# Decay rows of a bidirectional SSD encoder: stored by unit, both directions side by side, and fetched in 4 KB runs

## The chip, the cores and the metric

The kernel runs on one core of a Trainium2 chip. A core has a matrix engine (PE in the profile, with PEld for its weight loads), a vector engine (DVE), a scalar engine (ACT), GpSimd (POOL) and a queue engine (SP) that issues nearly all transfers between device memory and on-chip memory; 16 DMA engines carry them. Each engine works through its own list of instructions in order and waits on semaphores for the others. The metric is device microseconds (us) of one execution, lower is better. Before the change three runs gave 3012.8, 3020.76 and 3021.59 us; the median is 3020.76 us.

## What is computed

One encoder layer is applied to two sequences, 1024 and 2048 tokens, 1024 wide, all in float32. The input is normed and multiplied by a large matrix `w_in`. One part of the product goes through a Fourier mixing branch, another through a state-space branch that runs over the tokens in both directions; the two are gated, joined, projected and added to the input. The change concerns the state-space branch, computed in chunks of 128 tokens:

```
a = (dt * A)                                  # per token and head, one set for each direction
a_cs = cumsum(a, axis=chunk)
seg = a_cs[:, :, :, None] - a_cs[:, :, None, :]
decay = exp(where(lower triangle, seg, -inf))
cb = einsum('bclgn,bcsgn->bclsg', Cc, Bc)
y_diag = einsum('bclsg,bclsgr,bcsgrp->bclgrp', cb, decay, X)
...                                           # states of the chunks, carried from chunk to chunk
y_off = einsum('bclgn,bcgrpn,bclgr->bclgrp', Cc, prev, exp(a_cs))
y = y_fwd + flip(y_bwd) + D * xs              # 24 heads of 64 channels, in 4 groups
```

For each head, direction and chunk the kernel needs two rows of 128 numbers: `a_cs` along the chunk, laid over all 128 partitions (for `decay`), and `exp(a_cs)`, laid over the head's 64 partitions (for `y_off`). These are the decay rows.

## The kernel before, in words

The tokens are worked on in three blocks of 1024 (P for the first sequence, S1 and S2 for the second). In each block the projection is done in columns of 128 channels: a Job loads a 512 KB slice of `w_in` (`weights_in`, L182, one buffer `wr`), ACT rounds it into a high part `wh` (L189), POOL forms the rest `wl` (L190), and PE multiplies in three pieces of 342 tokens, 24 matmuls a piece (L361). One piece is a step. Everything else is hung on numbered steps, `pre` ahead of the step's matmuls or `post` behind them, and each engine gets its instructions in that order. So the order of the work on every engine, the SP queue included, is written out by these step numbers; no engine can take a later thing first.

The 24 heads are handled two at a time as 12 units, of 128 channels each. Ahead of the units, `dt_rows` turns the sums of a block into `rows` and `erow`, which hold one head and direction per partition (forward heads on partitions 0 to 23, backward on 32 to 55), and `dt_out` (L499, L500) writes both to device memory, as `ROWd` and `EXPd` in the order chunk, head, token. From there they are read back with each row repeated over many partitions, which is what `bcast_rows` does. `Unit.plan` places the work of a unit:

- four times (p = 0 to 3, two chunks each): `rows_in` asks for the rows of both directions (L540, tiles `R0` and `R1`, one request each), two steps later `rows_cut` masks them on POOL (L548), one step after that `rows_exp` takes eight exponentials on ACT (L558), then `rows_joined` adds the directions and multiplies by `cb` on DVE (L563, L564), and `diag` uses the result on PE (L575)
- `weighted` on POOL (L587, tile `xw`) and `states` on PE (L607, tile `pst`) and DVE (L614, L618): the states of the chunks
- twice (chunks 0 to 3 and 4 to 7): `decays` asks for the exponentiated rows (L635, tiles `er0` and `er1`, two requests for each direction), `across` uses them on DVE (L652), `gated` finishes on POOL (L658; in S1 also L662 and L663), `out` stores (L667, L669)

While block P or S1 is running, the input of the next one is brought in: `load_x` (L122, tile `xt`) for the sums of squares on ACT (L719), and again at the end of the block for the norm on DVE (L250) and the turn on PE (L264).

After the three blocks come the Fourier stage and two stages with the remaining products (from L839 on), which the change doesn't touch.

Of the kernel before, what the change touches and what calls it, by code (L numbers as in the profile page):

```python
# [9 lines left out]
F32 = mybir.dt.float32  # L10
# [8 lines left out]
P = 128  # L19
# [37 lines left out]
def tile_hybrid_encoder(ctx: ExitStack, tc: tile.TileContext, a):  # L57
# [37 lines left out]
    def bcast_rows(src, n):  # L95
        return src.partition_broadcast(n)
# [5 lines left out]
    with ExitStack() as ph:  # L102
# [61 lines left out]
        wdt = cp.tile([P, KT, 2, 64], F32R, name="wdt")  # L164

        def dt_weights_in():
            wdr = sp.tile([P, KT, 64], F32, tag="R1", bufs=3, name="wdr")
# [70 lines left out]
        def x_normed(b, i, xn):  # L238

            xt, n = xn  # L240
            if b["n"] == "P":
                junk = sp.tile([P, DM], BF16, tag="R0", bufs=3, name="junk")
# [7 lines left out]
            V.scalar_tensor_tensor(xt[:n, :], xt[:n, :], rs, nwb[:n, :], op0=ALU.mult, op1=ALU.mult)  # L250
# [175 lines left out]
        def dt_turned(B):  # L426
            B.pv = sp.tile([P, NCH, 64], F32, tag="xw", name="pv")
            for c4 in range(0, NCH, 4):
# [3 lines left out]
                S.copy(B.pv[:, c4:c4 + 4, :], pt[:, :, 0:64])  # L432
                V.tensor_tensor(B.pv[:, c4:c4 + 4, :], pt[:, :, 64:128], B.pv[:, c4:c4 + 4, :], op=ALU.add)

        def dt_softplus(B, part):

            pv = B.pv
            if part:
                dtm, dmx, de, dz = B.sp
                for m in (9, 7, 5, 3):  # L440
                    V.scalar_tensor_tensor(dtm, dtm, 1.0 / m, dz, op0=ALU.add, op1=ALU.mult)
                V.scalar_tensor_tensor(dtm, dtm, 1.0, de, op0=ALU.add, op1=ALU.mult)
                V.scalar_tensor_tensor(dtm, dtm, 2.0, dmx, op0=ALU.mult, op1=ALU.add)
# [4 lines left out]
            dtm = sp.tile([P, NCH, 64], F32, tag="R1", bufs=3, name="dtm")  # L448
            dmx = sp.tile([P, NCH, 64], F32, tag="R0", bufs=3, name="dmx")
            de = sp.tile([P, NCH, 64], F32, tag="R0", bufs=3, name="de")  # L450
            dz = sp.tile([P, NCH, 64], F32, tag="R1", bufs=3, name="dz")
# [44 lines left out]
            B.rows, B.erow = rows, erow  # L496

        def dt_out(B):
            nc.sync.dma_start(ROWd[B.bi].rearrange("c h l -> h c l"), B.rows)  # L499
# [25 lines left out]
        class Unit:  # L525
# [6 lines left out]


            def rows_in(self, p):
                B, u, cc = self.B, self.u, 2 * p
                self.R[p] = []
                for d in range(2):
                    hc = 32 * d + 2 * u
                    R = sp.tile([P, 2, 2, P], F32, tag=f"R{d}", bufs=3, name=f"R{d}")
                    nc.sync.dma_start(  # L540
                        R.rearrange("p c h l -> p c (h l)"),
                        bcast_rows(ROWd[B.bi][cc:cc + 2, hc:hc + 2, :].rearrange("c h l -> c (h l)"), P))
                    self.R[p].append(R)

            def rows_cut(self, p):
                for d, R in enumerate(self.R[p]):
                    sgn = 1 if d == 0 else -1
                    G.affine_select(  # L548
                        out=R.rearrange("p c h l -> p (c h) l"), in_=R.rearrange("p c h l -> p (c h) l"),
                        pattern=[[0, 4], [sgn, P]], compare_op=ALU.is_ge, fill=NEG, base=0,  # L550
                        channel_multiplier=-sgn)

            def rows_exp(self, p):
                for d, R in enumerate(self.R[p]):
                    hc = 32 * d + 2 * self.u
                    for c in range(2):
                        for h in range(2):
                            S.activation(R[:, c, h, :], R[:, c, h, :], AF.Exp,  # L558
                                         bias=self.B.lb[:, 2 * p + c, hc + h:hc + h + 1])

            def rows_joined(self, p):
                E = self.R[p]
                V.tensor_tensor(E[0], E[0], E[1], op=ALU.add)  # L563
                V.tensor_tensor(E[0], E[0],  # L564
                                self.B.cb[self.g][:, 2 * p:2 * p + 2, :].unsqueeze(2).broadcast_to([P, 2, 2, P]),
                                op=ALU.mult)

            def diag(self, p):

# [3 lines left out]
                for c in range(2):  # L573
                    for h in range(2):
                        T.matmul(pd[h * 64:h * 64 + 64, c2 + c, :],  # L575
                                 lhsT=self.xm[c4][:, c2 + c, h * 64:h * 64 + 64],
                                 rhs=self.R[p][0][:, c, h, :], start=True, stop=True)
                if p % 2:
                    self.y[c4] = y = sp.tile([P, 4, P], F32, tag="y0", name="y")
                    V.scalar_tensor_tensor(y.rearrange("p c l -> p (c l)"), self.xT[:, c4 * P:(c4 + 4) * P],  # L580
# [58 lines left out]
            def across(self, c4):  # L639

# [3 lines left out]
                for d in (1, 0):  # L644
                    cs = [c for c in range(4) if B.entered(d, c4 + c)]
                    cr = slice(cs[0], cs[-1] + 1)
                    po = bank([P, 4, P], f"po{d}")
                    for c in cs:
                        T.matmul(po[:, c, :], lhsT=self.H[d][:, c4 + c, :],
                                 rhs=B.CT[self.g][:, (c4 + c) * P:(c4 + c + 1) * P], start=True, stop=True)  # L650
                    t = sp.tile([P, 4, P], F32, tag="y1", bufs=1, name="yt")
                    V.tensor_tensor(t[:, cr], po[:, cr], self.er[d, c4][:, cr], op=ALU.mult)  # L652
                    V.tensor_tensor(y[:, cr], y[:, cr], t[:, cr], op=ALU.add)  # L653

            def gated(self, c4):
# [2 lines left out]
                G.tensor_tensor(yf, yf, zT[:, tk], op=ALU.mult)  # L658
                if self.B.b["n"] == "S1":

                    er_b = self.er[1, c4]
# [9 lines left out]
            def plan(self, s0):  # L671
# [714 lines left out]
```

## Time and profile before

| What | Value |
|---|---|
| median of three runs | 3020.76 us |
| the profiled execution, by its own time | 3021.5 us |
| its span from first to last instruction | 3019.7 us |
| PE, PEld, DVE, ACT, POOL busy | 94%, 85%, 73%, 46%, 49% of the span |
| mean granted clock of PE | 0.974 |
| DMA packets, bytes | 454578, 440.54 MB |
| three blocks with the units | about 130 to 1950 us |
| Fourier stage and remaining products | about 1950 us to the end |

A share of busy time is a mean over the whole span. PE is the engine nearest to full; where it is idle, the views of waits and the timeline name what ended each wait. The row of windows gives, for a stretch of time, the busy time of each engine, the clock granted to PE (1.00 is full), the busy share of the 16 DMA engines and the bytes that they moved. The rows themselves stand in the prediction.

### The profile page before, as it was taken

The page shows a single profiled execution, that of the slowest core. Times are in us where ns is not written, and L with a number is a line of the kernel's source. Part 1 is how long each engine was busy: PE and PEld are TensorE (multiplying, and loading weights), DVE is VectorE, ACT ScalarE, POOL GpSimd, SP SyncE. Part 2 cuts the span into 40 slices and gives each one's busy share as a digit, 9 for nine tenths or more (in the row PEclk, how much of TensorE's full clock was granted, in tenths as well). Part 3 has the DMA queues.
Part 4 walks back from the last instruction along what each step waited for, and adds up shares of the span by engine and source line. Part 5 has one row for each costly group of instructions (what it writes and reads, how often), then busy time and mean ns, then how long its engine had stood idle before and what let it go on. Part 6 is the DMA issues. An engine that isn't in the chain of part 4 may idle for free. (4 is left out here: it accounts for less than half of the span.)

```text
span 3019.7 us, 47067 instructions
## 1 busy us (share of the span) xinstructions
PE 2831.3 (94%) x17252; PEld 2570.1 (85%) x17252; DVE 2217.9 (73%) x3412; ACT 1389.5 (46%) x2980; POOL 1488.2 (49%) x1114
## 2 busy tenths in 40 slices
PE   6999999989999989989999999978899899989998
PEld 6899999989999889989999999867677677768887
DVE  3687777666778667666868777687989888866665
ACT  4544545434545454434544444334433533355554
POOL 1255646432567566542556564455787688610000
PEclk9999999999999999999999999979999999999999
DMA  3388877872789779853677687666553654352221
GB/s 97 77 130 160 167 156 170 139 142 78 143 163 171 164 188 155 160 153 74 122 164 144 154 160 137 127 217 235 168 181 130 231 166 147 126 199 91 94 85 69
DMA packets 454578, 440.54 MB, mean 146 GB/s; under 512 B 24384, under 2 KB 405444, under 8 KB 450508
## 3 DMA queue, kind: packets, MB, share of 16 engines
q1 hardware_dynamic: 454060, 436.50, 61.5%
q8 instruction: 136, 2.23, 0.3%
q14 instruction: 94, 0.77, 0.1%
q10 hardware_dynamic: 288, 1.05, 0.1%
HBM read 328.41 MB, written 110.10 MB: 145 GB/s over the span
## 5 line engine op out<-in xcount | busy, mean ns | idle before, releaser
L361 PE MATMUL ps<-uh,wh 128*128 128x342 f32 (+1 forms) x2880 | 962.3, 334 | 11.7 <-ACT uh L267 8.5
L361 PE MATMUL ps<-ul,wh 128*128 128x342 f32 (+1 forms) x2880 | 926.1, 322 | 2.5 <-DVE ul L268 2.5
L361 PE MATMUL ps<-uh,wl 128*128 128x342 f32 (+1 forms) x2880 | 927.2, 322 | 0.9 <-POOL wl L190 0.9
L190 POOL TENSOR_TENSOR wl<-wr,wh 128x1024 fp32r<-128x1024 f32 x120 | 298.9, 2491 | 712.2 <-ACT wh L189 698.6
L361 PEld LDWEIGHTS ps<-uh,wh 128*128 128x128 f32 x2880 | 551.2, 191 | 35.3 <-issue 16.0
L361 PEld LDWEIGHTS ps<-ul,wh 128*128 128x128 f32 x2880 | 553.6, 192 | 4.2 <-DVE ul L268 3.5
L361 PEld LDWEIGHTS ps<-uh,wl 128*128 128x128 f32 x2880 | 549.8, 191 | 1.7 <-POOL wl L190 1.6
L558 ACT ACTIVATE R<-R,lb 128x128 f32<-128x128 f32 x1152 | 356.1, 391 | 89.5 <-POOL R L548 88.0
L548 POOL TENSOR_SCALAR_AFFINE_SELECT R<-R 128x512 f32<-128x512 f32 x288 | 270.4, 954 | 117.0 <-DMA R<-ROWd 113.0
L618 DVE SCALAR_TENSOR_TENSOR H<-H,cd,pst 128x64 f32<-128x64 f32 x888 | 182.7, 275 | 92.6 <-PE pst L607 90.4
L587 POOL TENSOR_TENSOR xw<-xm,wd 128x512 f32<-128x512 f32 x144 | 188.6, 1319 | 74.1 <-ACT xm L423 62.5
L1102 PE MATMUL X<-whP,ah 128*128 128x512 f32 x480 | 195.2, 407 | 7.8 <-ACT pu L1111 5.4
L402 DVE SCALAR_TENSOR_TENSOR xT<-raw,cvt,xT 128x1024 f32<-128x1024 f32 x144 | 197.3, 1370 | 2.6
L367 ACT COPY raw<-ps 128x342 f32<-128x342 f32 x180 | 78.3, 438 | 252.9 <-PE ps L361 247.9
L1102 PE MATMUL X<-whP,al 128*128 128x512 f32 x480 | 192.1, 400 | 2.1 <-DVE al L1073 2.1
L1102 PE MATMUL X<-wlP,ah 128*128 128x512 f32 x480 | 193.1, 402 | 0.5 <-DVE wlP L861 0.5
L1214 POOL TENSOR_TENSOR ht<-ht,pu 128x512 f32<-128x512 f32 x96 | 155.4, 1627 | 62.9 <-ACT pu L1111 39.9
L607 PE MATMUL pst<-xw,Bm 128*128 128x128 f32 x1056 | 146.4, 281 | 28.6 <-POOL xw L587 28.6
L607 PEld LDWEIGHTS pst<-xw,Bm 128*128 128x128 f32 x1056 | 137.5, 195 | 33.8 <-POOL xw L587 33.6
L563 DVE TENSOR_TENSOR R<-R,R 128x512 f32<-128x512 f32 x144 | 141.3, 981 | 31.4 <-ACT R L558 28.8
L1073 DVE TENSOR_TENSOR al<-s,ah 128x512 fp32r<-128x512 f32 x144 | 143.6, 1019 | 20.2 <-ACT ah L1072 20.0
L653 DVE TENSOR_TENSOR y<-y,yt 128x512 f32<-128x512 f32 (+1 forms) x144 | 154.6, 1073 | 4.9
(264 smaller groups left out, 5665.4 us busy)
## 6 DMA issues: line engine op xcount, KB each, us to landing
R<-ROWd SPq DMA_DIRECT2D x288, 256.0 KB
wr<-in_w_in SPq DMA_DIRECT2D x120, 512.0 KB
er<-EXPd SPq DMA_DIRECT2D x288, 128.0 KB
Hd<-ht SPq DMA_DIRECT2D x48, 512.0 KB
ht<-Hd SPq DMA_DIRECT2D x48, 512.0 KB
y<-Yd SPq DMA_DIRECT2D x46, 512.0 KB
wlP<-WSd SPq DMA_DIRECT2D x21, 1024.0 KB
Yd<-y SPq DMA_DIRECT2D x72, 256.0 KB
```

The source lines that it names most:

```text
L190: G.tensor_tensor(wl, raw, wh.bitcast(F32), op=ALU.subtract)
L361: T.matmul(ps[:, :n], lhsT=wt[:, kt, :], rhs=ut[:, kt, :n], start=(i == 0), stop=(i == 3 * KT - 1))
L402: V.scalar_tensor_tensor(dst, raw[:, k:k + TB], cvt[:, 20 * k + ct:20 * k + ct + 1], dst, op0=ALU.mult, op1=ALU.add)
L548: G.affine_select(out=R.rearrange("p c h l -> p (c h) l"), in_=R.rearrange("p c h l -> p (c h) l"), pattern=[[0, 4], [sgn, P]], compare_op ...
L558: S.activation(R[:, c, h, :], R[:, c, h, :], AF.Exp, bias=self.B.lb[:, 2 * p + c, hc + h:hc + h + 1])
L587: G.tensor_tensor(xw, self.xm[c4].rearrange("p c (h e) -> p c h e", h=2), col(self.B.wd[:, c4:c4 + 4, hc:hc + 2]).broadcast_to([P, 4, 2, 6 ...
L607: T.matmul(pst[:, c, :], lhsT=B.Bm[self.g][:, c4 + c, :], rhs=xw[:, c, :, :].rearrange("p h e -> p (h e)"), start=True, stop=True)
L618: V.scalar_tensor_tensor(dst[:, e], H[d][:, cc, e], B.cd[:, cc, hc + h:hc + h + 1], pst[:, c, e], op0=ALU.mult, op1=ALU.add)
L653: V.tensor_tensor(y[:, cr], y[:, cr], t[:, cr], op=ALU.add)
L1073: V.tensor_tensor(al, src, ah.bitcast(F32), op=ALU.subtract)
L1102: T.matmul(ps, lhsT=at[:, k, :], rhs=wt[:, k, :], start=(first and i == 0), stop=(i == 11), skip_group_check=not first)
L1214: return lambda t: G.tensor_tensor(h, h, t, op=ALU.add)
```

## The change

`ROWd` and `EXPd` change their order in device memory. `ROWd` becomes [pair of chunks, head, direction, 256 numbers] and `EXPd` [half of the chunks, head, direction, 512 numbers], so that what one step of a unit reads (two heads, both directions, two chunks; or one head, both directions, four chunks) is one run of 4 KB. `rows_in` then makes one request of 512 KB into one tile `R` in place of two of 256 KB; `decays` makes two requests of 256 KB for a half of the chunks, into one tile `er`, in place of four of 128 KB. `dt_out` needs four requests in place of two. Inside `R` the order of a partition's numbers is head, direction, chunk, token, where it was chunk, head, token in a tile for each direction. The masks, the sum and the product take one direction of `R`, two runs of 256 numbers. The pools hold three `R` of 4 KB for three each of `R0` and `R1` of 2 KB; some small tiles that shared those buffers (`junk`, `wdr`, and the four tiles of `dt_softplus`, now two pairs) move with them.

```diff
-    ROWd = [dram.tile([NCH, 64, P], F32, name=f"ROWd{i}") for i in range(3)]
-    EXPd = [dram.tile([NCH, 64, P], F32, name=f"EXPd{i}") for i in range(3)]
+    ROWd = [dram.tile([4, 24, 2, 2 * P], F32, name=f"ROWd{i}") for i in range(3)]
+    EXPd = [dram.tile([2, 24, 2, 4 * P], F32, name=f"EXPd{i}") for i in range(3)]
...
+        def pair_of(name):
+            t = sp.tile([P, 2, NCH, 64], F32, tag="R", bufs=3, name=name)
+            return t[:, 0], t[:, 1]
...
         def dt_out(B):
-            nc.sync.dma_start(ROWd[B.bi].rearrange("c h l -> h c l"), B.rows)
-            nc.sync.dma_start(EXPd[B.bi].rearrange("c h l -> h c l"), B.erow)
+            for d in range(2):
+                for kept, src, n in ((ROWd, B.rows, 2), (EXPd, B.erow, 4)):
+                    nc.sync.dma_start(kept[B.bi][:, :, d, :].rearrange("p h x -> h p x"),
+                                      src[32 * d:32 * d + 24].rearrange("h (p c) l -> h p (c l)", c=n))
...
             def rows_in(self, p):
-                B, u, cc = self.B, self.u, 2 * p
-                self.R[p] = []
+                R = sp.tile([P, 2, 2, 2, P], F32, tag="R", bufs=3, name="R")
+                nc.sync.dma_start(
+                    R.rearrange("p h d c l -> p (h d c l)"),
+                    bcast_rows(ROWd[self.B.bi][p, 2 * self.u:2 * self.u + 2].rearrange("h d x -> (h d x)"), P))
+                self.R[p] = R
+
+            def rows_cut(self, p):
                 for d in range(2):
-                    hc = 32 * d + 2 * u
-                    R = sp.tile([P, 2, 2, P], F32, tag=f"R{d}", bufs=3, name=f"R{d}")
-                    nc.sync.dma_start(
-                        R.rearrange("p c h l -> p c (h l)"),
-                        bcast_rows(ROWd[B.bi][cc:cc + 2, hc:hc + 2, :].rearrange("c h l -> c (h l)"), P))
-                    self.R[p].append(R)
...
             def rows_joined(self, p):
-                E = self.R[p]
+                E = [self.R[p][:, :, d].rearrange("p h c l -> p h (c l)") for d in range(2)]
                 V.tensor_tensor(E[0], E[0], E[1], op=ALU.add)
...
-            def decays(self, d, c4):
-
-                hc = 32 * d + 2 * self.u
-                er = sp.tile([P, 4, P], F32, tag=f"er{d}", bufs=2, name=f"er{d}")
+            def decays(self, c4):
+
+                er = sp.tile([P, 2, 4, P], F32, tag="er", bufs=2, name="er")
                 for h in range(2):
-                    nc.sync.dma_start(er[h * 64:h * 64 + 64],
-                                      bcast_rows(EXPd[self.B.bi][c4:c4 + 4, hc + h, :], 64))
-                self.er[d, c4] = er
+                    nc.sync.dma_start(
+                        er[h * 64:h * 64 + 64].rearrange("p d c l -> p (d c l)"),
+                        bcast_rows(EXPd[self.B.bi][c4 // 4, 2 * self.u + h].rearrange("d x -> (d x)"), 64))
+                self.er[c4] = er
...
-                for d in (1, 0):
-                    pre(s0 + 11, self.decays, d, 0)
-                    pre(s0 + 13, self.decays, d, 4)
+                pre(s0 + 11, self.decays, 0)
+                pre(s0 + 13, self.decays, 4)
```

Each engine's list can be read from the two programs. First the SP queue in block P, from the last step of unit 0 to the first steps of unit 1, before the change (`R` are the rows for the masks, `er` the exponentiated rows, `wr` a slice of `w_in`; behind the arrow stands the source, then the shape; x2 means twice in a row):

```order
L540 DMA R_1225<-ROWd_67 128x2x256
L540 DMA R_1227<-ROWd_67 128x2x256
L635 DMA er_1272<-EXPd_70 64x4x128 x2
L635 DMA er_1275<-EXPd_70 64x4x128 x2
L182 DMA wr<-in_w_in 128x8x128
L635 DMA er_1386<-EXPd_70 64x4x128 x2
L635 DMA er_1389<-EXPd_70 64x4x128 x2
L540 DMA R_1400<-ROWd_67 128x2x256
L540 DMA R_1402<-ROWd_67 128x2x256
L540 DMA R_1494<-ROWd_67 128x2x256
L540 DMA R_1496<-ROWd_67 128x2x256
L182 DMA wr<-in_w_in 128x8x128
```

The same place of the SP queue after the change:

```order
L540 DMA R<-ROWd_67 128x1024
L633 DMA er<-EXPd_70 64x1024 x2
L182 DMA wr<-in_w_in 128x8x128
L633 DMA er<-EXPd_70 64x1024 x2
L540 DMA R<-ROWd_67 128x1024 x2
L182 DMA wr<-in_w_in 128x8x128
```

The places of `wr` among them are the same; between two of them stand half as many requests, each with twice the bytes. Second, POOL in the same block, around two masks (`wl` is the low part of the weights, `xw` the weighted inputs of the states, `ws` a part of later weights). Before:

```order
L190 TENSOR_TENSOR wl<-wr,wh 128x1024
L548 AFFINE_SELECT R_2227<-R_2227 128x512
L548 AFFINE_SELECT R_2229<-R_2229 128x512
L217 TENSOR_TENSOR ws<-wb 128x256
L218 TENSOR_TENSOR ws<-wb,ws 128x256
L190 TENSOR_TENSOR wl<-wr,wh 128x1024
```

After:

```order
L190 TENSOR_TENSOR wl<-wr,wh 128x1024
L549 AFFINE_SELECT R<-R 128x2x256 x2
L217 TENSOR_TENSOR ws<-wb 128x256
L218 TENSOR_TENSOR ws<-wb,ws 128x256
L190 TENSOR_TENSOR wl<-wr,wh 128x1024
```

Nothing moved; the two masks now work on one tile, in two runs of 256. On PE, ACT and DVE the lists have the same operations in the same places as well.

More of the change, by code (lines that the diff above doesn't have):

```diff
@@ L166, in dt_weights_in @@
         def dt_weights_in():
-            wdr = sp.tile([P, KT, 64], F32, tag="R1", bufs=3, name="wdr")
+            wdr = sp.tile([P, KT, 64], F32, tag="R", bufs=3, name="wdr")
             V.memset(wdr, 0.0)
@@ L241, in x_normed @@
             if b["n"] == "P":
-                junk = sp.tile([P, DM], BF16, tag="R0", bufs=3, name="junk")
+                junk = sp.tile([P, DM], BF16, tag="R", bufs=3, name="junk")
                 ss = sp.tile([P, 1], F32, tag="ss", name="ss")
@@ L447, in dt_softplus @@
                 return
[L448 to L451, printed above, removed]
+            dtm, dmx = pair_of("dtm")
+            de, dz = pair_of("de")
             V.tensor_scalar(dmx, pv, 0.0, None, op0=ALU.max)
@@ L534, in rows_in @@
             def rows_in(self, p):
-                B, u, cc = self.B, self.u, 2 * p
-                self.R[p] = []
-                for d in range(2):
-                    hc = 32 * d + 2 * u
-                    R = sp.tile([P, 2, 2, P], F32, tag=f"R{d}", bufs=3, name=f"R{d}")
-                    nc.sync.dma_start(
-                        R.rearrange("p c h l -> p c (h l)"),
-                        bcast_rows(ROWd[B.bi][cc:cc + 2, hc:hc + 2, :].rearrange("c h l -> c (h l)"), P))
-                    self.R[p].append(R)
-            def rows_cut(self, p):
-                for d, R in enumerate(self.R[p]):
+                R = sp.tile([P, 2, 2, 2, P], F32, tag="R", bufs=3, name="R")
[4 more added lines that the diff above has]
+            def rows_cut(self, p):
+                for d in range(2):
+                    R = self.R[p][:, :, d]
                     sgn = 1 if d == 0 else -1
[L548 to L551, printed above, removed]
+                    G.affine_select(out=R, in_=R, pattern=[[0, 2], [0, 2], [sgn, P]], compare_op=ALU.is_ge, fill=NEG,
+                                    base=0, channel_multiplier=-sgn)
             def rows_exp(self, p):
-                for d, R in enumerate(self.R[p]):
+                R = self.R[p]
+                for d in range(2):
                     hc = 32 * d + 2 * self.u
@@ L557, in rows_exp @@
                         for h in range(2):
-                            S.activation(R[:, c, h, :], R[:, c, h, :], AF.Exp,
+                            S.activation(R[:, h, d, c, :], R[:, h, d, c, :], AF.Exp,
                                          bias=self.B.lb[:, 2 * p + c, hc + h:hc + h + 1])
             def rows_joined(self, p):
-                E = self.R[p]
+                E = [self.R[p][:, :, d].rearrange("p h c l -> p h (c l)") for d in range(2)]
                 V.tensor_tensor(E[0], E[0], E[1], op=ALU.add)
-                V.tensor_tensor(E[0], E[0],
-                                self.B.cb[self.g][:, 2 * p:2 * p + 2, :].unsqueeze(2).broadcast_to([P, 2, 2, P]),
-                                op=ALU.mult)
+                cb = self.B.cb[self.g][:, 2 * p:2 * p + 2, :].rearrange("p c l -> p (c l)")
+                V.tensor_tensor(E[0], E[0], cb.unsqueeze(1).broadcast_to([P, 2, 2 * P]), op=ALU.mult)
             def diag(self, p):
@@ L576, in diag @@
                                  lhsT=self.xm[c4][:, c2 + c, h * 64:h * 64 + 64],
-                                 rhs=self.R[p][0][:, c, h, :], start=True, stop=True)
+                                 rhs=self.R[p][:, h, 0, c, :], start=True, stop=True)
                 if p % 2:
@@ L651, in across @@
                     t = sp.tile([P, 4, P], F32, tag="y1", bufs=1, name="yt")
-                    V.tensor_tensor(t[:, cr], po[:, cr], self.er[d, c4][:, cr], op=ALU.mult)
+                    V.tensor_tensor(t[:, cr], po[:, cr], self.er[c4][:, d, cr], op=ALU.mult)
                     V.tensor_tensor(y[:, cr], y[:, cr], t[:, cr], op=ALU.add)
@@ L659, in gated @@
                 if self.B.b["n"] == "S1":
-                    er_b = self.er[1, c4]
+                    er_b = self.er[c4][:, 1]
                     G.tensor_tensor(er_b, er_b, col(elt[:, c4:c4 + 4, self.u]).broadcast_to([P, 4, P]), op=ALU.mult)
```

## The prediction, made before the changed kernel ran

> **What bounds the kernel now.** I read the page first.
>
> ```profile
> PE 2831.3 (94%) x17252; PEld 2570.1 (85%) x17252; DVE 2217.9 (73%) x3412; ACT 1389.5 (46%) x2980; POOL 1488.2 (49%) x1114
> ...
> R<-ROWd SPq DMA_DIRECT2D x288, 256.0 KB
> ...
> er<-EXPd SPq DMA_DIRECT2D x288, 128.0 KB
> ```
>
> PE is busy 94% of the span, so a faster transfer pays only where PE stands still or runs slowly. Next comes the split of the span into windows: start and end, length, busy time of PE, PEld, DVE, ACT and POOL, granted clock, DMA share, GB/s. The middle row is the stage that the change touches.
>
> ```profile
> 0.00:130.00 130.00, 100.35 (x599) 95.47 (x600) 66.83 (x96) 58.82 (x105) 18.82 (x15) 0.95 0.31 82
> 130.00:1950.00 1820.00, 1755.49 (x12235) 1695.42 (x12234) 1317.48 (x2246) 862.16 (x1968) 979.09 (x757) 0.98 0.74 146
> 1950.00:3019.70 1069.70, 975.46 (x4422) 779.17 (x4421) 833.58 (x1071) 468.48 (x909) 490.30 (x343) 0.96 0.45 153
> ```
>
> In this stage PE is idle for 1820 - 1755.49 = 64.5 us, and its clock is not always full. That is all there is to win. What ended the idle time is in the view of PE's waits for the same window (total, times, longest):
>
> ```profile
> PE pst L607 <- POOL xw L587: 28.6, 18, 6.9
> PE pt L264 <- DVE H L618: 13.6, 4, 5.6
> PE pt L264 <- DVE xt L250: 6.3, 2, 5.7
> PE ptt L421 <- DVE y L580: 4.6, 2, 3.3
> PE pd L575 <- issue: 3.3, 1, 3.3
> ```
>
> No transfer is named, so each has to be followed back. The longest `pst` wait, from the timelines of ACT, POOL and PE (start, length; in brackets the idle time and what ended it):
>
> ```profile
> 1117.11 1.05 ACT L189 CAST wh<-wr 128x1024 fp32r<-128x1024 f32 x1 [6.22 <-DMA wr<-in_w_in]
> ...
> 1118.24 2.35 POOL L190 TENSOR_TENSOR wl<-wr,wh 128x1024 fp32r<-128x1024 f32 x1 [4.47 <-ACT wh L189]
> ...
> 1124.13 2.58 POOL L587 TENSOR_TENSOR xw<-xm,wd 128x512 f32<-128x512 f32 x2
> ...
> 1125.24 1.01 PE L607 MATMUL pst<-xw,Bm 128*128 128x128 f32 x3 [6.88 <-POOL xw L587]
> ```
>
> `wr` came late, ACT stood before it for 6.22 us, POOL's list ran late behind ACT, and PE paid 6.88 us. The longest `xt` wait, from SP, DVE and PE:
>
> ```profile
> 622.68 3.65 SPq L540 DMA_DIRECT2D R<-ROWd  x4
> 626.38 2.95 SPq L122 DMA_DIRECT2D xt<-in_x_sample  x1
> ...
> 646.52 1.28 DVE L250 SCALAR_TENSOR_TENSOR xt<-xt,ss,nwb 114x1024 f32<-114x1024 f32 x1 [12.42 <-DMA xt<-in_x_sample]
> ...
> 647.96 1.82 PE L264 MATMUL pt<-ident,xt 114*128 114x114 f32 x8 [5.72 <-DVE xt L250]
> ```
>
> Four requests for `R` stand ahead of `xt` in the queue, and `xt` lands some 20 us after its issue. How fast those rows move is in three short windows:
>
> ```profile
> 151.00:157.00 6.00, 6.00 (x42) 6.00 (x41) 5.97 (x13) 4.41 (x10) 4.50 (x3) 1.00 0.67 71
> 626.00:639.00 13.00, 13.00 (x98) 12.62 (x97) 7.77 (x8) 6.29 (x14) 5.48 (x5) 1.00 1.01 77
> 2666.00:2667.00 1.00, 1.00 (x6) 0.81 (x5) 1.00 (x2) 0.00 (x0) 1.00 (x1) 1.00 0.79 201
> ```
>
> From 626 to 639 four `R` requests fill all 16 engines (share 1.01) and move 77 GB/s x 13 us = 1.0 MB, exactly their size: 3.3 us each, 6.5 us a pair. The first window is mostly `er`, at 71 GB/s. So a unit, four pairs and 1 MB of `er`, occupies the queue for 4 x 6.5 + 1 MB / 71 GB/s = 26 + 15 = 41 us, and 36 units have 1820 us, 50.6 us each. **The queue of the transfers is close to full, and what stands in it behind the decay rows is late.**
>
> **The change, part by part.** Sums are made against the profiled execution's 3021.5 us, 0.7 us above the median of the runs.
>
> *The requests.* `R` becomes 4 x 36 = 144 requests with 128 runs of 4 KB, `er` 144 with 64 runs of 4 KB; the bytes stay. What a 4 KB row repeated over 128 partitions costs is shown by one transfer in the last stage, `fn`, 512 KB, just the shape of the new `R`:
>
> ```profile
> 2661.21 0.32 SPq L858 DMA_DIRECT2D wlP<-WSd  x1
> 2661.58 0.42 SPq L1271 DMA_DIRECT2D fn<-in_final_norm_w  x1
> ```
>
> It follows 1 MB of `wlP` in the queue, and 2666 to 2667, quoted above, lies in its passage: 201 GB/s, with little of others in it. I take 200 GB/s; bounds are 77 (no gain) and 238, the total at the start while the other such row, `nwb`, shared the engines:
>
> ```profile
> 3.00:5.00 2.00, 0.00 (x0) 0.00 (x0) 0.00 (x0) 0.00 (x0) 0.00 (x0) 1.00 0.90 238
> ```
>
> At 200 a new `R` takes 2.6 us for 6.5, the `er` of a unit 5 us for 15: 41 us becomes 16 us a unit. `xt` in the example stood behind 13 us of `R`; behind 5 us it comes 8 us sooner and PE's 5.72 us are gone. The same queue holds `wr`, wanted 6.22 us sooner above.
>
> *What PE gets back.* The five rows of waits sum to 28.6 + 13.6 + 6.3 + 4.6 + 3.3 = 56.4 us; the other 8.1 us I leave. ACT's waits in this window say what stands behind them:
>
> ```profile
> ACT xt L719 <- DMA xt<-in_x_sample: 58.9, 16, 9.9
> ACT wh L189 <- DMA wr<-in_w_in: 52.2, 29, 6.2
> ```
>
> *The clock.* After a wait PE runs slowly for a while. These matmuls follow the 3.33 us `ptt` wait, first at half clock, then full:
>
> ```profile
> 407.27 0.49 PE L361 MATMUL ps<-uh,wl 128*128 128x340 f32 x1
> 407.56 0.49 PE L361 MATMUL ps<-uh,wh 128*128 128x340 f32 x1
> ...
> 410.82 0.31 PE L361 MATMUL ps<-uh,wh 128*128 128x340 f32 x1
> 410.97 0.32 PE L361 MATMUL ps<-ul,wh 128*128 128x340 f32 x1
> ```
>
> They start 0.29 us apart, then 0.15: a half-clock us loses 0.45 us or a little more. Ten windows of 20 us hold all such stretches of the stage; these are the first, the third and the last:
>
> ```profile
> 140.00:160.00 20.00, 17.59 (x115) 16.64 (x114) 18.38 (x32) 12.52 (x30) 13.13 (x9) 0.91 0.57 114
> ...
> 460.00:480.00 20.00, 17.24 (x113) 16.38 (x112) 9.74 (x22) 12.96 (x27) 11.43 (x10) 0.91 0.92 210
> ...
> 1435.00:1455.00 20.00, 16.28 (x96) 15.73 (x95) 17.22 (x30) 12.87 (x32) 14.02 (x9) 0.83 0.62 119
> ```
>
> Over the stage the clock column gives (1 - 0.98) x 1820 = 36 us of lost clock, 27 to 45 by its rounding; the ten lose 0.09 to 0.26 of 20 us each, 31 us in all, which I take. That is 62 us at half clock; an estimated quarter falls inside the waits, so 62 x 0.75 x 0.45 = 21 us.
>
> The wait within 460 to 480 is this one:
>
> ```profile
> 468.43 0.84 PE L607 MATMUL pst<-xw,Bm 128*128 128x128 f32 x3 [2.76 <-POOL xw L587]
> ```
>
> The Trainium skill, "TensorE: Matmul & The Clock Gate", Part 1, says that PE falls to half clock after an idle window of about 3.4 us. By that rule only the longer waits would cost clock, an estimated 15 us in place of 21. Here 2.76 us were enough (0.91 in its window), so the trace doesn't bear the rule's length out.
>
> *The sum.* 56.4 + 21 = 77 us can go. Not all of it will: the places of `wr` and `xt` in the lists stay, some `pst` waits of 0.3 us are POOL's own chain, and an engine that is early at one place waits at the next. Between none and all I choose two thirds, since the relief (25 us a unit, 8 us in the example) is larger than each single wait: 77 x 0.65 = **50 us**.
>
> *Costs.* The masks and the sum now read two runs of 256. Rows for them, on DVE with minimum/median/maximum in ns, on POOL with count, busy us, mean ns and idle time before; `xw` is a POOL operation over many short runs:
>
> ```profile
> L563 DVE TENSOR_TENSOR R<-R,R x142: 680/692/2023, 131.1 to 1941.3; 128x512 f32<-128x512 f32 x142
> L564 DVE TENSOR_TENSOR R<-R,cb x142: 691/1003/2772, 131.8 to 1942.3; 128x512 f32<-128x512 f32 x142
> ...
> L548 POOL TENSOR_SCALAR_AFFINE_SELECT R<-R 128x512 f32<-128x512 f32 x286 | 269.1, 956 | 110.1 <-DMA R<-ROWd 106.1 <-DVE yt L652 4.0
> L587 POOL TENSOR_TENSOR xw<-xm,wd 128x512 f32<-128x512 f32 x144 | 188.6, 1319 | 74.1 <-ACT xm L423 62.5 <-PE pst L607 10.7 <-DMA wr<-in_w_in 0.9
> ```
>
> On DVE, L564 already reads a broadcast in pieces, and its minimum is 11 ns above L563's: nothing. For a mask the far bound is `xw`, 1319 ns against 956: 0.36 us, twice ahead of each of 18 `pst` waits, 13 us; the near one is nothing, which I take, since POOL is busy for only 979 of 1820 us. A faster mask isn't excluded by a row, but POOL's idle time would hide it. `dt_out` issues four requests for two, three times:
>
> ```profile
> 115.90 0.69 SPq L499 DMA_DIRECT2D ROWd<-rows  x1
> ```
>
> At 0.69 us that is at most 3 x 2 x 0.69 = 4 us of SP, ahead of rows wanted two steps later; nothing, up to 4 us if that cover is gone, nothing below, as it adds requests. The shared buffers of `junk`, `wdr` and `dt_softplus` leave each engine's list as it was: nothing. No wait is added. A pair's first mask now waits for both halves; this is the third rival.
>
> 3021.5 - 50 = 2971.5 by the profiled execution, 2971 against the median.
>
> **The rivals.** *Only a part comes back* (a gain of 10 to 35 us, middle 3000): POOL's and ACT's lists, not the transfers, hold the next wait. For it: POOL's chain of 2.35 + 2.58 us and three operations between them stand ahead of `pst` in the quoted example, whatever `wr` does. Against it: the wait began with 6.22 us for a transfer.
>
> *Long runs don't help.* All partitions read the same bytes, and `er` with 0.5 KB runs moves 71 GB/s where `R` with 1 KB runs moves 77, so the length of a run did little there. If the rate stays, the queue holds 41 us a unit as before, and only issues are saved: 3018, within 0.3%. Against it speaks `fn`. The Trainium skill, "DMA: Bandwidth & Descriptors", Specifications, puts the line rate at transfers of 512 B and more; by it the old runs were long enough and nothing is won. The 77 GB/s at 1 KB disagree with it.
>
> *Slower.* If the rate stays, a further thing bites: a mask of the forward rows could start 3.3 us before the backward rows landed; now both wait for 512 KB, and POOL ends one mask, 0.956 us in the row of masks above, later. It decides below 512 KB / (6.5 - 0.95) us = 94 GB/s. Put on each of the 26 waits in the five rows, with the same share of clock (21/56), it is 26 x 0.95 x 1.4 = 34 us: 3055. Against it: the new rate would have to be under half of what `fn` shows.
>
> **How the numbers follow.** A measurement of this kernel can tell about 0.3%, 9 us, from no change. The forecast (gain of 35 to 80 us) has 0.62, a part 0.18, no help 0.12, slower 0.08. The range reaches from 2938, all 77 us and some of the 8.1 left aside, to 3010, where 11 us come back: that leaves out the last two cases. Faster 0.80, same 0.12, slower 0.08.
>
> **What would show it.** The request rows should read 144 of 512 KB and 144 of 256 KB; a window with `R` alone should move about 200 GB/s; the stage's DMA share should fall from 0.74 to below 0.55; POOL's wait for `R` from 106 us to below 30, ACT's for `wr` and `xt` to less than half; PE's idle time in the stage from 64.5 to about 30 us, with a clock of 0.99. A rate near 77 GB/s would make the forecast wrong; so would transfers that land early while `pst` and `pt` still wait.

## Result and profile after

| | before | after |
|---|---|---|
| median, us | 3018.89 (3012.80 to 3021.59, 4 runs) | 2938.65 (2933.68 to 2938.98, 4 runs) |
| profiled execution, its own time / span, us | 3021.5 / 3019.7 | 2938.98 / 2937.0 |

After / before is **0.9733, 95% interval 0.9714 to 0.9752**: 80 us faster. From the page after the change, the engines' busy time and the requests:

```profile
PE 2806.8 (96%) x17252; PEld 2551.2 (87%) x17252; DVE 2223.1 (76%) x3412; ACT 1382.3 (47%) x2980; POOL 1515.5 (52%) x1114
...
R<-ROWd SPq DMA_DIRECT2D x144, 512.0 KB
...
er<-EXPd SPq DMA_DIRECT2D x144, 256.0 KB
```

The requests are halved in number and doubled in size. To see where the 82.7 us of span went, I cut both executions at the same instruction of the program, the start of the last `pd` that waits for `H` in the stage of the units: at 1953 us before, at 1876.3 after. Windows before (start and end, length, busy time of PE, PEld, DVE, ACT, POOL, clock, DMA share, GB/s):

```profile
130.00:1953.00 1823.00, 1756.41 (x12243) 1696.17 (x12241) 1320.44 (x2254) 863.66 (x1972) 979.55 (x757) 0.98 0.74 146
1953.00:3019.70 1066.70, 974.54 (x4414) 778.42 (x4414) 830.61 (x1063) 466.98 (x904) 489.85 (x342) 0.96 0.45 153
```

The same two stretches after:

```profile
130.00:1876.30 1746.30, 1732.59 (x12239) 1677.44 (x12239) 1324.92 (x2250) 854.82 (x1965) 1004.13 (x755) 1.00 0.51 153
1876.30:2937.00 1060.70, 974.98 (x4414) 779.52 (x4414) 829.78 (x1063) 466.84 (x904) 490.55 (x342) 0.96 0.45 152
```

The stage is 76.7 us shorter. PE's idle time in it fell from 1823 - 1756.41 = 66.6 to 1746.3 - 1732.59 = 13.7 us, which is 52.9 us; the other 23.8 us are busy time that went away for the same matmuls, and with them the clock rose from 0.98 to 1.00. The part behind the stage is 6.0 us shorter. PE's waits in the stage after (total, times, longest), the first four:

```profile
PE pst L606 <- POOL xw L586: 3.4, 9, 0.9
PE pt L264 <- DVE H L617: 2.6, 2, 2.0
PE ps L361 <- DVE zT L273: 2.3, 1, 2.3
PE pd L574 <- DVE H L617: 2.1, 1, 2.1
```

`pst` went from 28.6 to 3.4 us, `pt` behind `H` from 13.6 to 2.6, and `pt` behind `xt`, `ptt` behind `y` and `pd` behind "issue" left the list. On the way there, ACT's waits for `wr` (52.2 us before) have no row any more, and that for `xt` is one of 1.6 us. What ACT and POOL wait for now, from 130 to 1950 us:

```profile
ACT raw L367 <- PE ps L361: 323.2, 119, 5.0
...
POOL xw L586 <- ACT xm L423: 107.8, 34, 5.0
```

This wait of ACT for PE's results grew from 230.5 to 323.2 us, and POOL's for `xm`, which ACT copies out of PE's results, from 62.5 to 107.8. The engines that PE used to wait for now wait for PE, or for each other behind PE.

One window shows the new rate. After the change, from 120 to 123 us, `R` requests almost alone:

```profile
120.00:123.00 3.00, 3.00 (x23) 3.00 (x22) 2.65 (x2) 0.68 (x1) 1.41 (x2) 1.00 1.01 313
```

313 GB/s, where before it was 77 in the window that the prediction quotes.

### The profile page after: what moved, and what is told of

Read it like the earlier page. It is cut to its first block, busy times and chain, and to the rows that moved or that the text cites. A ratio compares the mean times of both kernels' runs of the same rounds, so it can differ in the third digit from the quotient of the medians.

```text
span 2937.0 us, 46503 instructions
## 1 busy us (share of the span) xinstructions
PE 2806.8 (96%) x17252; PEld 2551.2 (87%) x17252; DVE 2223.1 (76%) x3412; ACT 1382.3 (47%) x2980; POOL 1515.5 (52%) x1114
## 5 line engine op out<-in xcount | busy, mean ns | idle before, releaser
L361 PEld LDWEIGHTS ps<-uh,wh 128*128 128x128 f32 x2880 | 545.2, 189 | 36.5 <-issue 15.5
L652 DVE TENSOR_TENSOR y<-y,yt 128x512 f32<-128x512 f32 (+1 forms) x144 | 161.3, 1120 | 5.0
L272 ACT ACTIVATE zT<-ps 128x342 f32<-128x342 f32 (+1 forms) x108 | 49.1, 454 | 219.0 <-PE ps L361 218.7
L565 DVE TENSOR_TENSOR R<-R,cb 128x512 f32<-128x512 f32 x144 | 148.4, 1030 | 5.0
L651 DVE TENSOR_TENSOR yt<-po,er 128x512 f32<-128x512 f32 (+1 forms) x144 | 91.2, 634 | 76.0 <-PE po L648 67.8
```

The source lines that it names most:

```text
L361: T.matmul(ps[:, :n], lhsT=wt[:, kt, :], rhs=ut[:, kt, :n], start=(i == 0), stop=(i == 3 * KT - 1))
L565: V.tensor_tensor(E[0], E[0], cb.unsqueeze(1).broadcast_to([P, 2, 2 * P]), op=ALU.mult)
```

## The experiments

The theory of the prediction came first: the rows were slow because their runs were short; 4 KB runs are fast, the queue empties, and PE's waits end. Its rivals: the number of requests counts, not the runs; or it is the place in memory that the runs lie at. Each run was timed together with runs of before. These lay between 2997.57 and 3018.48 us, so ratios are compared, each to the runs of before timed with it. The gain in us, worked out from the ratios, differs with them: 80 us above, 73 for e4, which is the changed kernel but for a gap on chip, and 67 for e12, which is the changed kernel itself.

| Run | Memory order | Pieces of R, er | R, GB/s | us | Ratio, 95% interval |
|---|---|---|---|---|---|
| e1_rows_only | R new, er old | 4 KB, 0.5 KB | | 2942.92 | 0.9790 (0.9720 to 0.9860) |
| e2_exp_only | R old, er new | 1 KB, 4 KB | | 2960.75 | 0.9849 (0.9780 to 0.9919) |
| e3_merged_short_runs | old, half the requests | 1 KB, 0.5 KB | 77 | 3096.80 | 1.0302 (1.0230 to 1.0374) |
| e4_one_place_short_pieces | new | 1 KB, 0.5 KB | 317 | 2932.62 | 0.9756 (0.9687 to 0.9824) |
| e5_by_unit_2kb | new, directions apart | 2 KB, 2 KB | 161 | 2937.78 | 0.9753 (0.9692 to 0.9814) |
| e6_before_odd_step | old, step 34 KB for 32 | 1 KB, 0.5 KB | 251 | 2937.05 | 0.9751 (0.9696 to 0.9806) |
| e8_merged_odd_step | as e3, step 34 KB | 1 KB, 0.5 KB | 290 | 2938.49 | 0.9756 (0.9697 to 0.9814) |
| e10_step_36kb | old, step 36 KB | 1 KB, 0.5 KB | 270 | 2937.90 | 0.9774 (0.9752 to 0.9796) |
| e11_step_48kb | old, step 48 KB | 1 KB, 0.5 KB | 79 | 2981.97 | 0.9920 (0.9894 to 0.9946) |

"Step" is the distance in device memory between the chunks that one request reads. Two further kinds of run, e7 and e9 with e12, follow at the end.

**Each half alone.** e1 takes the change for `ROWd` and `R`, e2 the one for `EXPd` and `er`; the rest is as before.

```diff
-    ROWd = [dram.tile([NCH, 64, P], F32, name=f"ROWd{i}") for i in range(3)]
+    ROWd = [dram.tile([4, 24, 2, 2 * P], F32, name=f"ROWd{i}") for i in range(3)]
```

> The R part of the change alone (4 KB runs for the masks' rows), the er part as before. If the rate of the rows fills the queue: a unit's rows take about 4 x 2 us + 15 us = 23 us of the queue in place of 41, under half of a unit's 50 us, so most of the 80 us come back: about 2955 us, and POOL's wait for R falls from 106 us to under 30. If instead the two requests for er, which stand right ahead of wr and R, do the harm, it stays within 20 us of before (3000 or more).

And e2:

```diff
-    EXPd = [dram.tile([NCH, 64, P], F32, name=f"EXPd{i}") for i in range(3)]
+    EXPd = [dram.tile([2, 24, 2, 4 * P], F32, name=f"EXPd{i}") for i in range(3)]
```

> The er part of the change alone (4 KB runs for the exponentiated rows), R as before. By the filled queue: 26 us + 5 us = 31 us of 50 a unit, so a smaller part comes back: about 2990 us, with POOL's wait for R at 60 us or more. If er does the harm: 2960 or less.

By their ratios e1 gains 63 us of its 3005 and e2 45: together 108, but the whole change gives 80, or 73 by e4, which was timed with them. So the gain is not a sum of the two: either half frees most of what was late, and the second half finds little left. e2 gave more than I expected, 2990 us with 60 us or more of POOL's wait for `R`. It took 2960.75, just above the 2960 that I had set for the rival by which `er` does the harm. With `er` alone made faster, most of POOL's wait for `R` is gone, so the rate of `R` was not all of that wait: the `er` that stood ahead of it had a part. But e1, where `R` alone was made faster, gave more still. In the group of POOL's masks (count, busy, mean ns, idle time before and what ended it), for e2 in the window 130 to 1880 us, some waiting for `R` is left:

```profile
L551 POOL TENSOR_SCALAR_AFFINE_SELECT R<-R 128x512 f32<-128x512 f32 x282 | 275.8, 998 | 18.3 <-DMA R<-ROWd 18.3
```

And among PE's waits of e2 in that window:

```profile
PE pst L610 <- POOL xw L590: 10.2, 12, 3.4
```

The slow `R` still costs 10.2 us at `pst` there; with e1, where `er` is the slow one, the same wait is 3.5 us.

**Fewer requests, old order in memory.** e3 asks as often as the changed kernel does, but reads the old memory order: `R` as four runs of 1 KB that lie 16 KB apart (two directions, two chunks), `er` as eight of 512 B. It has the merged tiles, the masks in two runs and the shared buffers too.

```diff
-                for d in range(2):
-                    hc = 32 * d + 2 * u
-                    R = sp.tile([P, 2, 2, P], F32, tag=f"R{d}", bufs=3, name=f"R{d}")
...
+                R = sp.tile([P, 2, 2, 2, P], F32, tag="R", bufs=3, name="R")
+                rows = ROWd[self.B.bi][cc:cc + 2].rearrange("c (d h) l -> (c d) (h l)", d=2)
+                nc.sync.dma_start(
+                    R.rearrange("p c d h l -> p (c d) (h l)"),
+                    bcast_rows(rows[:, 2 * self.u * P:(2 * self.u + 2) * P], P))
```

> As many requests as the changed kernel (144 and 144), but ROWd and EXPd in the order of before, so that an R request is four runs of 1 KB, 16 KB apart, for each partition, and an er request eight of 512 B. Theory of the run (long runs in one place are what is fast): the rate stays near 77 GB/s and the time near before, 3010 to 3030 us. Theory of the count (fewer requests are what helps): 2940 to 2965 us.

It is 3% slower than before. The rate of `R`, in its window from 121 to 130 us, stayed what it was:

```profile
121.00:130.00 9.00, 9.00 (x65) 9.00 (x65) 3.94 (x5) 2.21 (x5) 2.19 (x3) 1.00 0.35 77
```

And its waits on POOL, ACT and PE in the stage, from 130 to 1950 us:

```profile
POOL R L549 <- DMA R<-ROWd: 154.8, 58, 9.0
...
ACT wh L189 <- DMA wr<-in_w_in: 168.2, 55, 7.0
...
PE pst L607 <- POOL xw L587: 62.3, 32, 5.2
```

POOL now waits up to 9.0 us for a pair that must land whole (4.7 before), ACT waits 168.2 us for `wr` in place of 52.2, and `pst` 62.3 us in place of 28.6. So fewer requests bring nothing while the rows stay in this order. That the time got worse, which neither theory had forecast, is not only that a pair must land whole: the first `er` went more slowly than before, at 32 GB/s from 152 to 158 us in e3 and 71 from 151 to 157 before. How much each of the two costs was not taken apart.

**Short pieces from one place.** e4 is the kernel after the change, but the tiles on chip get a gap of 16 B between the runs, so the transfer goes in pieces of 1 KB and 512 B again; the bytes still lie side by side in device memory.

```diff
-                R = sp.tile([P, 2, 2, 2, P], F32, tag="R", bufs=3, name="R")
+                R = sp.tile([P, 4, 2 * P + 4], F32, tag="R", bufs=3, name="R")[:, :, 0:2 * P]
```

> Memory order and requests of the changed kernel, but the tiles on the chip have 16 bytes between pieces of 1 KB (R) and 512 B (er), so that the 4 KB of one place are moved in pieces as short as before. Theory of the piece's length: 77 GB/s, 3010 to 3030 us. Theory of the place (what matters is that a request's bytes lie side by side in memory, over which the partitions' reads spread): about 2940 to 2960 us, with a rate of R well over 100 GB/s.

Its window from 120 to 123 us:

```profile
120.00:123.00 3.00, 3.00 (x21) 3.00 (x20) 2.38 (x2) 0.94 (x1) 1.39 (x2) 1.00 1.04 317
```

Pieces of 1 KB move 317 GB/s when they come from one place. **The length of the pieces was not the cause.**

**2 KB runs, directions apart.** e5 keeps the 288 and 288 requests; each reads one run of 2 KB.

```diff
-    ROWd = [dram.tile([NCH, 64, P], F32, name=f"ROWd{i}") for i in range(3)]
-    EXPd = [dram.tile([NCH, 64, P], F32, name=f"EXPd{i}") for i in range(3)]
+    ROWd = [dram.tile([4, 2, 24, 2 * P], F32, name=f"ROWd{i}") for i in range(3)]
+    EXPd = [dram.tile([2, 2, 24, 4 * P], F32, name=f"EXPd{i}") for i in range(3)]
```

> Rows by unit, but each direction apart: runs of 2 KB, and as many requests as before (288 and 288). Theory of the place (the rate grows with how many bytes that lie side by side a request repeats: 77 GB/s at 1 KB, over 250 at 4 KB): about 150 GB/s, a unit's rows 21 us of the queue in place of 41, about 2945 us. If it takes the joining of both directions to get the gain: 2980 or more.

Its window from 121 to 124 us:

```profile
121.00:124.00 3.00, 3.00 (x23) 3.00 (x23) 2.23 (x3) 1.74 (x3) 3.00 (x1) 1.00 0.94 161
```

Half the rate of the changed kernel, and the whole gain within the intervals. So the two directions need not lie together, and above some rate between 77 and 161 GB/s a faster one buys nothing more here that these runs can show. The rate itself was forecast at about 150: with 77 GB/s for 1 KB side by side, 161 for 2 KB and 313 for 4 KB, it grows nearly in proportion to the bytes that lie side by side. The next run shows that lying side by side is not the only way to such a rate. Whether the two requests of a pair, whose places are 24 KB apart in e5, also slow each other was not tested.

**The kernel before with another step.** e6 changes nothing but the addresses. Each direction of a chunk gets 34 rows where it had 32: the chunks lie 34 KB apart and not 32, the directions 17 KB and not 16. Requests, pieces, tiles, masks and sums are those of before; only `dt_out` needs four requests for two.

```diff
-    ROWd = [dram.tile([NCH, 64, P], F32, name=f"ROWd{i}") for i in range(3)]
-    EXPd = [dram.tile([NCH, 64, P], F32, name=f"EXPd{i}") for i in range(3)]
+    ROWd = [dram.tile([NCH, 2, 34, P], F32, name=f"ROWd{i}") for i in range(3)]
+    EXPd = [dram.tile([NCH, 2, 34, P], F32, name=f"EXPd{i}") for i in range(3)]
```

> The kernel before, runs of 1 KB and 512 B and all requests as before, but in memory a chunk's rows lie 34 KB after those of the chunk before in place of 32, and the directions 17 KB apart in place of 16. If the slow rate comes from the even step (the places of a request fall on one part of the memory that can't serve them side by side): two places of 1 KB give about 150 GB/s and four of 512 B at least as much, 2940 to 2965 us. If a place of 1 KB is slow by itself, wherever the next one lies: 77 GB/s and 3000 to 3015 us as before.

2937.05 us, the same gain as the change within the intervals. The number of packets and the bytes stand on the page of e6:

```profile
DMA packets 454674, 440.54 MB, mean 150 GB/s; under 512 B 24480, under 2 KB 405540, under 8 KB 450604
```

454674 packets and 440.54 MB, against 454578 and 440.54 MB before. In two windows of e6, `R` from 121 and `er` from 153 us:

```profile
121.00:124.00 3.00, 3.00 (x24) 3.00 (x23) 2.75 (x2) 0.57 (x1) 2.13 (x3) 1.00 0.77 251
...
153.00:156.00 3.00, 3.00 (x26) 2.79 (x24) 2.96 (x10) 1.38 (x5) 0.00 (x0) 1.00 1.16 252
```

251 and 252 GB/s, where before `R` moved 77 and `er` 71. (In the last us of the second window `R` already follows; its first two alone move 249.) e8 does the same to the slow e3 (its rows in memory get the step of e6):

> e3_merged_short_runs (four runs of 1 KB in an R request, eight of 512 B in an er request) with the places 17 KB apart in place of 16. By the theory of the even step: four places side by side, 250 to 330 GB/s, 2930 to 2950 us, some 150 us under e3. If many short places are slow by themselves: near e3, 3090.

Its ratio is 0.9756 where that of e3 is 1.0302, 2938.49 us where e3 took 3096.80, for 1 KB more between two directions. Its window:

```profile
121.00:124.00 3.00, 3.00 (x24) 3.00 (x23) 2.42 (x2) 0.91 (x1) 0.92 (x2) 1.00 0.86 290
```

**Which steps are slow.** e10 and e11 are e6 with 36 and 48 rows for 34.

> The kernel before with a chunk step of 36 KB (9 x 4 KB) in place of 32, directions 18 KB apart. If only a large power of two as step is slow: R above 200 GB/s as with 34 KB, POOL's wait for R below 10 us, about 2938 us. If every multiple of 4 KB clashes: R near 77 GB/s and about 3019 us.

> The kernel before with a chunk step of 48 KB (3 x 16 KB), directions 24 KB apart. If only a power of two is slow: about 2938 us. If every multiple of 16 KB (the same lower 14 address bits) is slow: R near 77 GB/s and about 3019 us. Between, if 32 KB is needed for the full clash.

A window within the first `R` requests of e10, and one of e11:

```profile
119.00:121.00 2.00, 2.00 (x15) 2.00 (x14) 2.00 (x2) 0.08 (x1) 1.42 (x2) 1.00 0.93 270
```

```profile
121.00:124.00 3.00, 3.00 (x22) 3.00 (x21) 2.23 (x3) 1.88 (x3) 0.25 (x1) 1.00 0.93 79
```

At 36 KB the rate is there, at 48 KB `R` is as slow as at 32. So a power of two is not needed: 16 KB (e3), 32 and 48 KB are slow, 34 and 36 KB are fast. e11 still gained 23 us (0.8%). Its `er` is faster than before: from 157 to 161 us it moved 93 GB/s, where before it was 71. In e6, e10 and e11 the distance between the two directions changed with the step (17, 18 and 24 KB for 16), so whether the places within one request or those of requests that run side by side must not clash is not taken apart.

**The weights in another queue.** e7 leaves the rows as before and lets ACT's queue ask for `wr` (`slot[0]` is the number of the step; what is asked for ahead of step 1 stays with SP), to see whether the place behind the rows is what makes `wr` late.

```diff
-            nc.sync.dma_start(raw, w_in[:, c0:c0 + P].rearrange("(k p) c -> p k c", p=P))
+            (nc.scalar if slot[0] else nc.sync).dma_start(raw, w_in[:, c0:c0 + P].rearrange("(k p) c -> p k c", p=P))
```

> The kernel before, rows and rate as before, but the slices of w_in (wr) are asked for by ACT and so wait in ACT's queue, not behind the rows in SP's. Theory of the queue (wr is late since it stands behind the rows): PE's wait for xw falls from 28 us to under 12, with its part of the clock, and 25 to 40 us come back: 2965 to 2985 us; the waits for xt stay. If the slow rows hold up every transfer, in whatever queue: 3000 or more.

3165.73 us, ratio 1.0510 (1.0428 to 1.0592). Its first wait on ACT:

```profile
ACT wh L189 <- DMA wr<-in_w_in: 397.9, 74, 15.7
```

ACT waits 397.9 us for `wr` over the whole span, 56.2 before. The request now stands in ACT's own list, behind ACT's work and its waits, and a second thing changed with the queue. So the run says nothing about the theory of the queue, only that this place for the request is worse.

**The start.** With the stage at a nearly full clock, the first 130 us hold PE's largest waits for a transfer. e9 is the kernel after the change, with each load of 114 rows of `x` made as 112 and 2 rows; e12 is the kernel after the change once more, on the same chip.

```diff
-            eng.dma_start(xt[:n, :], a["x"][b["seq"]][r0:r0 + n, :])
+            for lo, hi in ((0, 112), (112, n)):
+                if hi > lo:
+                    eng.dma_start(xt[lo:hi, :], a["x"][b["seq"]][r0 + lo:r0 + hi, :])
```

> The kernel after the change, with each load of 114 rows of x made as 112 and 2 rows. If the first waits of PE (for xt 14.4 us, for uh behind it 9.6 us) are the load's rate, and 112 rows are spread over more engines: xt's window at the start above 200 GB/s in place of about 155, and 4 to 8 us gained, about 2932 us. If the start is bound by ACT and DVE or by the sum of bytes: within 2 us of the kernel after.

> The kernel after the change once more, as the companion of the run with x loaded in two parts on the same chip: 2938 us, ratio 0.973.

e9 took 2935.74 us, ratio 0.9767 (0.9750 to 0.9784); e12 2938.86, ratio 0.9777 (0.9761 to 0.9793). PE's two largest waits from 0 to 130 us, in e12 and then in e9:

```profile
PE pt L264 <- DVE xt L250: 14.3, 3, 11.9
PE ps L361 <- ACT uh L267: 8.4, 3, 6.4
```

```profile
PE pt L266 <- DVE xt L252: 12.9, 3, 10.6
PE ps L363 <- ACT uh L269: 4.8, 3, 3.6
```

The two waits are 5.0 us shorter in these executions, but the intervals of the ratios overlap. From 8 to 20 us the transfers moved 171 GB/s in e9 and 149 in e12, less than the 200 that I had put on a spread over more engines. Whether splitting the load pays is open, and no run here is faster than the change by more than its interval. The ratio of e12, 0.9777, is not the 0.973 expected of it: the runs of before timed with it took 3005.17 us, 14 less than in the result, while the changed kernel's own time was the same.

## Why the prediction was right in its path and wrong in its reason

**The queue close to full.** Right. e6 leaves the work of PE, ACT, POOL and DVE as it was, changes the rate at which the same requests pass, and brings the whole gain; POOL's wait for `R` fell in it to 3.2 us from 130 to 1880 us, as it did in the changed kernel, whose group of masks reads:

```profile
L549 POOL TENSOR_SCALAR_AFFINE_SELECT R<-R 128x512 f32<-128x512 f32 x285 | 272.5, 977 | 5.2 <-DMA R<-ROWd 5.2
```

5.2 us for 106.1. So slow rows were what made the rest late. That the rest was late because it stood behind them in one queue, and not because it shared the 16 engines with them, was read from the order of the requests; e7 was to show it and doesn't.

**The new rate, 200 GB/s.** It was more, 313 in the window above. The reason that I gave by calling these "long runs" failed. `fn`, from which I took the rate, is a row from one place, and that it is one place was what counted: 1 KB pieces from one place move 317 GB/s (e4), and at steps of 34 and 36 KB 251 and 270 (e6, e10). That the change which I took for longer runs also put the bytes in one place was luck. It did not hurt the number, but I would have advised 4 KB runs where 2 KB of padding do.

**The sum of 77 us.** It stood: 52.9 us of idle time and 23.8 us of busy time make 76.7 us in the stage. That it is so near is in part luck, since the five rows of waits gave 56.4 - 6.0 = 50.4 us, other rows 2.5, and the clock 2.8 us more than the 21 that I gave it. By the rule that I weighed there, the Trainium skill's "TensorE: Matmul & The Clock Gate", Part 1, the clock's part would have been an estimated 15 us. The trace after the change doesn't bear out the length of its idle window either. This is the window from 1250 to 1270 us:

```profile
1250.00:1270.00 20.00, 17.95 (x127) 17.30 (x126) 16.63 (x41) 8.67 (x20) 8.75 (x8) 0.91 0.71 200
```

PE's one wait in it is 2.0 us, `pt` behind `H`, and the clock is 0.91.

**The share of two thirds.** This is the term that was mis-sized: 77 x 0.65 = 50 should have been 77 x 1.0. So 2938.65 us lies 32 us below the forecast of 2971 and only 0.65 us inside the lower end of its range, 2938; one of the four runs, 2933.68, lies below it. I argued that an engine which is early at one place waits at the next. It does, but what it waits for is PE: the rows of ACT and POOL in the result. Nothing late took the place of the transfers, and e1 and e2 show why: the relief was so far beyond need that half of it brought 63 or 45 us, where e4, timed with them, brought 73. POOL's own chain, for which I left part of the `pst` waits, kept 3.4 of 28.6 us.

**The part behind the stage.** I counted it as unchanged; it gave 6.0 us. Nearly all is one wait. PE's first wait behind the stage, before:

```profile
PE pm L972 <- DVE Ue L985: 15.8, 1, 15.8
```

And after:

```profile
PE pm L970 <- DVE Ue L980: 10.4, 1, 10.4
```

In the other runs it goes along with the rows: 22.6 us in e3, 12.7 in e11, 10.6 in e6. What DVE was held by there was not followed.

**The costs.** In the stage, the mask's mean was 977 ns in place of 956: 285 x 0.021 = 6 us on POOL, beside its idle time, near the bound of nothing and far from 1319. The two runs of 256 are not shown to cost even that: in e6, whose masks have the shape of before, the mean is 978. DVE's rows after:

```profile
L565 DVE TENSOR_TENSOR R<-R,cb 128x512 f32<-128x512 f32 x143 | 147.7, 1033 | 4.9
L563 DVE TENSOR_TENSOR R<-R 128x512 f32<-128x512 f32 x143 | 139.5, 976 | 5.9 <-issue 4.7 <-ACT R L558 1.1
```

1033 and 976 ns, against 1056 and 985 in the same view before: nothing. The shared buffers and the merged requests were not tried alone, but e8, which has them, and e6, which has not, are 1.4 us apart with intervals that overlap.

**The rivals.** "Only a part comes back" did not happen. "Long runs don't help" was right in its first half, that 0.5 and 1 KB runs moving alike speaks against the length, and wrong to conclude that the rate stays: the change also moved the bytes to one place. The rule named beside it, the Trainium skill's "DMA: Bandwidth & Descriptors", Specifications, which puts line rate at 512 B and more, I set aside for the 77 GB/s at 1 KB; e6 speaks for it, with 512 B pieces of `er` at 249 GB/s, and e4, with 1 KB pieces at 317. The "slower" rival did not come in this change, but its condition, a rate that stays while the pair must land whole, is e3, and e3 is slower, by 3.0% where I had worked out 34 us or 1.1%. (The five rows hold 27 waits and not 26, which makes it 36 us.) The mechanism that I gave it is at most a part of this: ACT's wait for `wr` and the slower `er` of e3 are not in it.

**The signs.** Requests, DMA share in the stage (0.51, below 0.55), POOL's wait and ACT's waits all came as written; the rate was 313 and not about 200 GB/s, PE's idle time fell to 13.7 us, not about 30, and the clock rose to 1.00, not 0.99. None of these signs could have told long runs from one place. A window of before with other 1 KB or 512 B pieces, read by all partitions from one place, might have.

**What stays open** is what makes places 16, 32 or 48 KB apart slow to read together. The Trainium skill, "DMA: Bandwidth & Descriptors", Latency and other measured facts, tells of copies that slow down when the rows of the partitions lie 2 MiB or more apart at a power of two, and that 4 KiB of padding restored the rate. That is for steps far larger than here and for different rows in each partition; the runs here show a like effect for a row that all partitions read, and that 2 KB of padding suffice. No run shows the mechanism.

## What to carry to other kernels

When a transfer that repeats the same rows over many partitions is slow, try other addresses before another shape: here two rows of padding in a scratch tensor gave all that a new layout, merged requests and new tiles gave. And when a queue that several engines depend on is relieved by far more than each single wait, count the whole sum of the waits and of the clock behind them, unless a row shows what will be late next; here nothing was.

## What the runs showed of the hardware beyond that

- The same row read by 128 partitions from two places in one request moves 77 GB/s at a step of 32 KB, 79 at 48 KB, 251 at 34 KB, 270 at 36 KB, with packets of the same size and nearly the same number; four places 16 KB apart also move 77 (e3), 17 KB apart 290 (e8).
- The share of the DMA engines does not tell how fast such a read goes. Before, 77 GB/s went with a share of 1.01; in e3 it went with 0.35, and in e11 79 GB/s with 0.93.
- Waits of PE below 7 us each, 52.9 us in all, cost another 23.8 us in matmuls at less than the full clock: taking them away gained nearly half as much again. A wait of 2.0 us, the only one in its window of 20 us, went with a clock of 0.91 there.
